# First MLP group of a gMLP/GLA layer step: up of two token blocks ahead of the third's, down by seven quadrant products, norm transposes later

## Chip, cores and metric

The kernel runs on one core of one Trainium2 chip. The metric is the device time of one launch in microseconds (us); the median of several launches counts.

## What is computed

One layer of an encoder step on 1056 tokens (1024 of a prompt, 32 of a running stream), model width 1024, all in fp32:

```python
def trunk_layer(x, c, s0, ...):
    mod = jax.nn.silu(c) @ w_ada + b_ada
    shift1, scale1, gate1, shift2, scale2, gate2 = split(mod, 6)
    h = x * (1.0 + scale1) + shift1
    mix, s_fin, v_rows = token_mixers(h, s0, ...)      # gated linear attention and gMLP
    x = layer_norm(DN_ALPHA * x + (1.0 + gate1) * (mix @ w_o + b_o), ln1_g, ln1_b)
    h2 = x * (1.0 + scale2) + shift2
    f = jnp.square(jax.nn.relu(h2 @ w_up + b_up)) @ w_down + b_down     # 1024 -> 4096 -> 1024
    x = layer_norm(DN_ALPHA * x + (1.0 + gate2) * f, ln2_g, ln2_b)
    return x, s_fin, v_rows
```

The change concerns the MLP (`w_up`, `w_down`) and what stands just ahead of it.

## The kernel before

**Tiles.** Tokens lie in three blocks: b = 0 and 1 of 384, b = 2 of 288 (256 and 32). Features lie on the partitions, so a tile of 128 features x 384 tokens is one matmul output. Every fp32 operand is split into a high and a low part (`hl`), and each product is three matmuls (`PASS`). A split is a CAST on ACT (L1024) and a subtraction on DVE (L1025).

**Stages around the change.** `out_proj_d(b)` computes the output projection (evicted to `y` by ACT, L936). `norm1(b)` turns `y` to rows (PE transposes, L1128), adds the residual, normalizes, turns back (PE transposes, L227), and forms `h2[b]`, eight feature tiles a block, as high and low part: ACT (L236) writes the high part, DVE (L233) the value, POOL (L239) the difference. Then the MLP runs in eight groups g of 512 of the 4096 features: up (1024 to 512, bias, relu, square) and down (512 to 1024, added into `acc`).

**Weights.** The class `W` loads raw weight tiles by DMA on SP (L1081) into four raw slots and splits them into eleven `hl` slots. A *unit* is 1024 numbers a partition in two slots. A *bundle* makes, from two units (A11, A12, A21, A22), also the sums that the Strassen-Winograd form needs (S1 to S4, on POOL, L1069 to L1072). `W.keep` holds slots back for others.

**Seven products.** In groups 1 to 7, blocks 0 and 1 are the two columns of a 2x2 matrix of quadrants, and up and down take seven products instead of eight (`Group.up` by the list `SEQ`, L1361; `Group.down` by `SEQ_DN`, L1428); block 2 is done plainly (`up_b2`, `down_b2`, L250 and L1222). The sums that up needs of `h2` (T1 to T4) are computed once by `t_prod` on POOL (L1257 to L1261), split, written to DRAM (`td`, by SP, L1267) and read back for each group through a ring of six slots (`ring`, issued by POOL, L1309). The sums that down needs of the group's own `f` are formed by `f_split`.

**Group 0** differs. Its up runs tile by tile through `up_std` (feature tiles m = 0, 1 for block 0, then for block 1, then block 2; then m = 2, 3 for all three), which squares on DVE (L1211) and splits f at once (L1212, L1213) into `f` and `fb2`. Its down is plain: for each of four weight units 12 matmuls for each of two outputs of each block (L1222), while `t_prod` makes the T products for the later groups.

**What sets the order.** PE's order is made by hand: `Order` runs generators by priority; each yields the PE time that it has issued and a delay until it wants its next turn (or a condition). `main_d` is the main stream, `norm1(b)` comes ahead of it when its delay has passed, `t_prod` behind it. The other engines are put in order when the program is built, by a scheduler that follows the tiles. Every engine then runs its queue strictly in that order.

Of the kernel before, what the change touches and what calls it, by code (L numbers as in the profile page):

```python
# [93 lines left out]
def cost(n):  # L94
    return max(n / 2.4, 106.0) + 2.0


def build(tc, io):
# [4 lines left out]
    with ctx:  # L103
# [9 lines left out]
        def mm():  # L113
            return cur["ps"].tile([P, 512], F32, tag="mm", name="mm", bufs=cur["mm"])
# [874 lines left out]
        with tc.tile_pool(name="pd", bufs=1, reuse_waits="tile") as pd, \  # L989
# [37 lines left out]
            class Weights:  # L1027
# [3 lines left out]
                def __init__(self):  # L1031
                    self.loads, self.steps, self.out, self.raw = [], [], {}, {}
                    self.keep = (0, 0)

# [39 lines left out]
                def pump(self):  # L1074
                    go = True
                    while go:
                        go = False
                        if self.loads and len(raws.free) > self.keep[0]:
                            key, u = self.loads.pop(0)
                            self.raw[key] = raws.take()  # L1080
                            DM.dma_start(self.raw[key], io["w"][u])  # L1081
                            go = True
                        if self.steps:
                            slot, f, k = self.steps[0]
                            if (k is None or k in self.raw) and (len(hls.free) > self.keep[1] if slot else halves.free):
# [23 lines left out]
            for m in range(4):  # L1109
                W.unit(("u", 0, m), U_UP + m)  # L1110
            for i in range(4):
                W.unit(("d", 0, i), U_DN + i)
            for g in range(1, 8):
                u, d = U_UP + 4 * g, U_DN + 4 * g
                W.bundle((("u", g, 0), (u, u + 2)), (("u", g, 1), (u + 1, u + 3)))
                if g < 7:
                    W.bundle(*((("d", g, r), (d + 2 * r, d + 2 * r + 1)) for r in range(2)))
                else:
                    for i in (0, 2, 1, 3):
                        W.unit(("d", 7, i), d + i)  # L1120
# [38 lines left out]
            def norm1(b):  # L1159
                tl = xr[b]  # L1160
                yield 0, 2500
                for wi, (off, n, _) in enumerate(WIN[b]):
# [38 lines left out]
            def up_std(hl, m, b, f):  # L1201
# [13 lines left out]
                yield from fm_tile(hl, h2[b], n, done)  # L1215

            def down_mm(pt, hl, q, f, n):

                for kk in range(4):
                    o_ = 256 * (kk % 2) + 128 * q  # L1220
                    for j, (a, c_) in enumerate(PASS):
                        PE.matmul(pt[:, :n], hl[kk // 2][:, a, o_:o_ + 128], f(kk)[:, c_],  # L1222
                                  start=(kk == 0 and j == 0), stop=(kk == 3 and j == 2))
# [22 lines left out]
            def t_prod():  # L1246

                yield lambda: h2[1] is not None
                for t, b, k0 in (("B11", 0, 0), ("B21", 0, 4), ("B22", 1, 4)):
                    for j in range(2):  # L1250
                        DM.dma_start(tv[t, j], h2[b][:, :, k0 + 2 * j:k0 + 2 * j + 2, :].bitcast(F32))
                for kk in range(4):
                    yield lambda: len(raws.free) >= 2 and len(hls.free) >= 2
                    r = [raws.take() for _ in range(2)]
                    b11, b12, b21, b22 = (r[i][:, 512 * j:512 * j + 384] for i in range(2) for j in range(2))
# [6 lines left out]
                    for t, src in (("T1", b11), ("T3", b12), ("T2", b22), ("T4", b21)):  # L1262
# [5 lines left out]
                        hls.give(h)  # L1268
                    for x_ in r:
                        raws.give(x_)  # L1270
                    yield 0, 9000
                W.keep = (0, 0)

# [27 lines left out]
            class Group:  # L1301
# [134 lines left out]
                def down_ev(self, prod, v, m):  # L1436
# [5 lines left out]
                    if prod == "P1":  # L1442
                        if self.g == 1:
# [86 lines left out]
            def main_d():  # L1530
# [14 lines left out]

                W.keep = (2, 3)
                yield lambda: h2[0] is not None
                tp = order.add(t_prod(), 7)
                f_a = [pd.tile([P, 2, 2, 768], F32R, tag="F", name="f", bufs=1)]

                def fa(m, b):
                    return f_a[m // 2][:, m % 2, :, 384 * b:384 * b + 384]
                hl = [W.unit_of("u", 0, m) for m in range(2)]
                for m in range(2):
                    yield from up_std(hl[m], m, 0, fa(m, 0))
                yield lambda: h2[1] is not None
                f_a.append(pd.tile([P, 2, 2, 768], F32R, tag="R", name="f", bufs=2))
                for m in range(2):
                    yield from up_std(hl[m], m, 1, fa(m, 1))
                yield lambda: h2[2] is not None  # L1560
                fb2 = pd.tile([P, 4, 2, 288], F32R, tag="R", name="fb2", bufs=2)
                for m in range(4):
                    if m > 1:
                        hl.append(W.unit_of("u", 0, m))
                        for b in range(2):
                            yield from up_std(hl[m], m, b, fa(m, b))
                    yield from up_std(hl[m], m, 2, fb2[:, m])
                    W.unit_done("u", 0, m)
# [4 lines left out]
                             .rearrange("p (a n) -> p a n", a=2) for i in range(3)]  # L1573
                groups = [Group(g) for g in range(8)]
                for gr in groups[1:]:
                    gr.queue()
                ring.pump()
                for i in range(4):
                    hl = W.unit_of("d", 0, i)
                    for b in range(3):  # L1580
                        for q in range(2):
                            pt = mm()
                            n = BLK[b][1]
                            down_mm(pt, hl, q, lambda kk: fb2[:, kk] if b == 2 else fa(kk, b), n)
                            down_ev(pt, 4 * (i % 2) + 2 * (i // 2) + q, ((b, 0, n),))
                            yield 12 * cost(n), 0
                    W.unit_done("d", 0, i)
                tmps_t = pd.tile([P, 8, 384], F32, tag="R", name="tmps", bufs=2)
                tmps = Slots([tmps_t[:, i] for i in range(6)])
                p1 = [tmps_t[:, 6], tmps_t[:, 7], pd.tile([P, 384], F32, name="p1")]  # L1590
                for g in range(1, 7):
# [111 lines left out]
```

## Time and profile before

| | us |
|---|---|
| three runs | 1233.87, 1240.7, 1239.12 (median 1239.12) |
| profiled execution | 1236.65, span 1234.9, mean granted clock 0.973 |
| busy: PE, weight load | 1171.4, 1116.4 |
| busy: DVE, ACT, POOL | 933.0, 531.9, 488.5 |
| 500 to 566 (group 0's up): PE busy, clock | 60.5 of 66, 0.87 |
| 566 to 612 (group 0's down): PE busy, clock | 46.0 of 46, 1.00 |
| 612 to 660 (group 1's up): PE busy, clock | 44.6 of 48, 0.96 |

Rows of a timeline give start, duration, engine, line, operation, output and inputs, shape, count; the brackets behind it give the idle time ahead of it and what ended that. Rows of windows give, after the stretch and its length, the busy time of PE, the weight load (PEld), DVE, ACT and POOL with their counts, then the granted TensorE clock (1.00 is full speed), the share of the DMA engines and GB/s. SPq is the DMA issue queue on SP.

### The profile page before, as it was taken

The numbers are of one execution on the slowest core, as the hardware profiler recorded it, in microseconds if no ns is written. First come the engines' busy times: TensorE is split into PE (matmuls) and PEld (weight loads), VectorE is DVE, ScalarE is ACT, GpSimd is POOL, SyncE is SP. The second block draws the span as 40 slices with busy tenths as digits, with TensorE's granted clock in tenths as the row PEclk, the third lists the DMA queues.
The fourth block names the chain that finished last, engine by engine and source line by source line (L and its number), as shares of the span: only waits on it lengthen the run. The fifth ranks groups of instructions, "written<-read, shape, count | busy, mean of one in ns | idle before, by whom it ended". The sixth has DMA issues, their size and how long they took to land.

```text
span 1234.9 us, 22104 instructions
## 1 busy us (share of the span) xinstructions
PE 1171.4 (95%) x8467; PEld 1116.4 (90%) x8467; DVE 933.0 (76%) x1906; ACT 531.9 (43%) x1087; POOL 488.5 (40%) x669
## 2 busy tenths in 40 slices
PE   5999997899899999899989999999999999999994
PEld 3679997798788899879989999999999999999994
DVE  5663899667888588767659769689598696796586
ACT  4462422544656577553334343343443443433221
POOL 3441224335665144448542442333324514432043
PEclk9999998899989999889999999999999999999998
DMA  9603456110102746304762563753825726637412
GB/s 373 222 2 133 154 207 219 50 37 3 40 2 72 279 126 227 126 18 150 264 251 69 195 242 97 242 180 117 301 94 190 254 79 216 234 102 248 146 49 93
DMA packets 49498, 188.46 MB, mean 153 GB/s; under 512 B 5328, under 2 KB 10928, under 8 KB 49392
## 3 DMA queue, kind: packets, MB, share of 16 engines
q1 hardware_dynamic: 35280, 109.97, 25.3%
q0 software_dynamic: 14112, 77.08, 18.0%
q8 instruction: 67, 1.10, 0.4%
q14 instruction: 39, 0.32, 0.1%
HBM read 171.36 MB, written 15.66 MB: 151 GB/s over the span
## 4 chain that ended last, share of the span: by engine, by line
PE 73%; DVE 12%; DMA 5%; POOL 3%; issue 2%; ACT 2%; SPq 0%; DVEq 0%; POOLq 0%; ACTq 0%
PE mm L250 22%; PE mm L1361 15%; PE mm L1428 13%; PE mm L1222 9%; PE zp L284 3%; PE mm L284 3%; DVE jk L883 2%; DVE hl L1025 2%; DMA raw<-in_w_dram 1%; DMA tdT<-hl 1%; DVE wad L883 1%; DMA wst<-in_w_dram 1%; DVE acc L1453 1%; PE zp L250 1%; PE mm L1128 1%
## 5 line engine op out<-in xcount | busy, mean ns | idle before, releaser
L1024 ACT CAST hl<-raw 128x512 fp32r<-128x512 f32 (+1 forms) x238 | 143.8, 613 | 238.8 <-PE mm L1428 94.6
L1025 DVE TENSOR_TENSOR hl<-raw,hl 128x512 fp32r<-128x512 f32 (+1 forms) x238 | 203.0, 859 | 36.5 <-ACT hl L1024 36.5
L1361 PE MATMUL mm<-ring,hl 128*128 128x384 f32 x960 | 172.8, 337 | 3.4 <-DMA ring<-tdT 3.4
L1361 PEld LDWEIGHTS mm<-ring,hl 128*128 128x128 f32 x960 | 167.7, 189 | 4.0 <-issue 3.2
L1428 PE MATMUL mm<-ring,hl 128*128 128x384 f32 x792 | 140.6, 335 | 1.1 <-DVE acc L1453 1.1
L1428 PEld LDWEIGHTS mm<-ring,hl 128*128 128x128 f32 x792 | 137.5, 188 | 1.4 <-ACT ring L1024 1.4
L250 PE MATMUL mm<-hT,whl 128*128 128x384 f32 (+1 forms) x792 | 132.3, 327 | 1.0 <-ACT mix L306 1.0
L250 PEld LDWEIGHTS mm<-hT,whl 128*128 128x128 f32 x792 | 129.7, 192 | 2.6 <-ACT mix L306 1.5
L250 PE MATMUL mm<-h,hl 128*128 128x288 f32 (+1 forms) x756 | 121.6, 317 | 1.9 <-POOL h L239 1.5
L250 PEld LDWEIGHTS mm<-h,hl 128*128 128x128 f32 x756 | 114.5, 195 | 4.8 <-POOL h L239 3.7
L1069 POOL TENSOR_TENSOR raw<-raw 128x512 f32<-128x512 f32 x26 | 37.2, 1432 | 183.6 <-DMA raw<-in_w_dram 161.3
L1453 DVE SCALAR_TENSOR_TENSOR acc<-mm,G,acc 128x384 f32<-128x384 f32 x162 | 93.8, 608 | 5.5 <-PE mm L1428 4.9
L1222 PE MATMUL mm<-fb,hl 128*128 128x288 f32 x708 | 97.0, 295 | 0.0
L1222 PEld LDWEIGHTS mm<-fb,hl 128*128 128x128 f32 x708 | 95.4, 189 | 0.0
L1233 DVE SCALAR_TENSOR_TENSOR acc<-mm,G,acc 128x256 f32<-128x256 f32 (+3 forms) x176 | 61.8, 390 | 12.3 <-PE mm L1222 12.2
L250 PE MATMUL mm<-mhl,hl 128*128 128x384 f32 (+1 forms) x384 | 65.1, 324 | 1.8 <-ACT hl L1024 1.8
L879 POOL TENSOR_TENSOR wad<-wad,csb 128x1024 f32<-128x1024 f32 x11 | 31.3, 2844 | 84.9 <-DVE jk L883 46.4
L284 PE MATMUL mm<-whl,hT 128*128 128x272 f32 (+1 forms) x384 | 55.3, 307 | 8.6 <-DVE whl L619 6.4
L284 PEld LDWEIGHTS mm<-whl,hT 128*128 128x128 f32 x384 | 53.2, 210 | 10.9 <-DVE whl L619 6.6
L250 PEld LDWEIGHTS mm<-mhl,hl 128*128 128x128 f32 x384 | 60.0, 192 | 2.6 <-ACT hl L1024 2.1
L1309 POOL DMA_DIRECT2D ring<-tdT x56 | 31.3, 560 | 73.0 <-PE mm L1361 42.1
L284 PE MATMUL zp<-zvw,hT 128*128 128x512 f32 x192 | 53.3, 423 | 4.5 <-ACT hT L236 4.5
(253 smaller groups left out, 2258.9 us busy)
## 6 DMA issues: line engine op xcount, KB each, us to landing
ring<-tdT POOLq DMA_DIRECT2D x56, 768.0 KB, 6.0
raw<-in_w_dram SPq DMA_DIRECT2D x80, 512.0 KB, 3.7
ring<-tdB POOLq DMA_DIRECT2D x42, 768.0 KB, 6.3
wst<-in_w_dram SPq DMA_DIRECT2D x34, 512.0 KB, 4.1
wad<-in_w_dram SPq DMA_DIRECT2D x32, 512.0 KB, 4.4
tdT<-hl SPq DMA_DIRECT2D x16, 384.0 KB, 3.0
st<-in_w_dram SPq DMA_DIRECT2D x10, 512.0 KB, 10.2
tdB<-h SPq DMA_DIRECT2D x6, 768.0 KB, 4.3
```

What stands on the lines that cost most here:

```text
L250: PE.matmul(pt[:, :n], h[:, a, 128 * kk:128 * kk + 128], act[:, b_, k, :n], start=(i == 0 and j == 0), stop=(i == 7 and j == 2))
L284: PE.matmul(pt[:n, :width], act[:, a, k, off:off + n], hl[:, b_, width * kk:width * kk + width], start=(k == 0 and a + b_ == 0), stop=(k = ...
L879: G.tensor_tensor(w, w, csb[:, c], ALU.mult)
L883: V.scalar_tensor_tensor(jk, w, 1.0, csb[:, c], ALU.mult, ALU.mult, accum_out=acc_)
L1024: S.copy(hl[:, 0, :n], src)
L1025: V.tensor_tensor(hl[:, 1, :n], src, hl[:, 0, :n].bitcast(F32), ALU.subtract)
L1069: G.tensor_tensor(s, a21, a22, ALU.add)
L1222: PE.matmul(pt[:, :n], hl[kk // 2][:, a, o_:o_ + 128], f(kk)[:, c_], start=(kk == 0 and j == 0), stop=(kk == 3 and j == 2))
L1233: V.scalar_tensor_tensor(ac, pt[:, o + lo - p0:o + hi - p0], G2[:, m, c:c + 1], ac, ALU.mult, ALU.add)
L1361: PE.matmul(pt[:, :384], hl[:, a, o_:o_ + 128], quad(ts[j])[:, b_, kk], start=first and j + kk + i == 0, stop=j + kk + i == 4, skip_group_ ...
L1428: PE.matmul(pt[:, :384], hl[:, a, o_:o_ + 128], f[:, b_, kk], start=first and kk + i == 0, stop=kk + i == 3, skip_group_check=True)
L1453: V.scalar_tensor_tensor(ac, v, G2[:, m, 0:1], ac, ALU.mult, ALU.add)
```

## The change

Group 0 now has the form of the later groups from its f on. Up of blocks 0 and 1 runs over all four feature tiles (`up_plain`: relu and square on ACT, f whole into one tile `F`), ahead of block 2's four tiles; down is `g0.down()`, which takes the seven products on `F` and block 2 plainly, first. Its four weight units become a bundle of two pairs (r = 0, 1); they may be loaded only after `t_prod` has taken two raw slots (`W.open`), and `t_prod` now keeps these two until all four of its steps kk are done. `norm1` waits twice as long before its first turn. `p1` (a product used in three places) is initialized by group 0 instead of group 1.

```diff
 def norm1(b):
     tl = xr[b]
-    yield 0, 2500
+    yield 0, 5000
...
+def up_plain(hl, m, b, f):
+    def done(pt):
+        t = tmp_tile("rl")
+        S.activation(t, pt[:, :384], AF.Relu, bias=col("b_up", m))
+        S.activation(f, t, AF.Square)
+    yield from fm_tile(hl, h2[b], 384, done)
...
# W: loading
-if self.loads and len(raws.free) > self.keep[0]:
+if self.loads and raws.free and (self.open or self.loads[0][0][0] != "d"):
...
-for i in range(4):
-    W.unit(("d", 0, i), U_DN + i)
-for g in range(1, 8):
+for g in range(8):
     u, d = U_UP + 4 * g, U_DN + 4 * g
-    W.bundle((("u", g, 0), (u, u + 2)), (("u", g, 1), (u + 1, u + 3)))
+    if g:
+        W.bundle((("u", g, 0), (u, u + 2)), (("u", g, 1), (u + 1, u + 3)))
     if g < 7:
         W.bundle(*((("d", g, r), (d + 2 * r, d + 2 * r + 1)) for r in range(2)))
...
# t_prod
+yield lambda: len(raws.free) >= 2
+r = [raws.take() for _ in range(2)]
+W.open = True
 for kk in range(4):
-    yield lambda: len(raws.free) >= 2 and len(hls.free) >= 2
-    r = [raws.take() for _ in range(2)]
+    yield lambda: len(hls.free) >= 2
...
-        for x_ in r:
-            raws.give(x_)
         yield 0, 9000
-W.keep = (0, 0)
+for x_ in r:
+    raws.give(x_)
+W.keep = 0
...
# main_d, after the output projection
-W.keep = (2, 3)
+W.keep = 3
...
-hl = [W.unit_of("u", 0, m) for m in range(2)]
-for m in range(2):
-    yield from up_std(hl[m], m, 0, fa(m, 0))
-yield lambda: h2[1] is not None
...
-for m in range(2):
-    yield from up_std(hl[m], m, 1, fa(m, 1))
+g0.f = pd.tile([P, 4, 768], F32, tag="F", name="F", bufs=1)
+hl = []
+for ms in ((0, 1), (2, 3)):
+    hl += [W.unit_of("u", 0, m) for m in ms]
+    for b in range(2):
+        yield lambda: h2[b] is not None
+        for m in ms:
+            yield from up_plain(hl[m], m, b, g0.f[:, m, 384 * b:384 * b + 384])
...
 for m in range(4):
-    if m > 1:
-        hl.append(W.unit_of("u", 0, m))
-        for b in range(2):
-            yield from up_std(hl[m], m, b, fa(m, b))
     yield from up_std(hl[m], m, 2, fb2[:, m])
     W.unit_done("u", 0, m)
 yield lambda: tp not in order.streams
...
-for i in range(4):
-    hl = W.unit_of("d", 0, i)
-    for b in range(3):
-        for q in range(2):
-            pt = mm()
-            n = BLK[b][1]
-            down_mm(pt, hl, q, lambda kk: fb2[:, kk] if b == 2 else fa(kk, b), n)
-            down_ev(pt, 4 * (i % 2) + 2 * (i // 2) + q, ((b, 0, n),))
-            yield 12 * cost(n), 0
-    W.unit_done("d", 0, i)
+yield from g0.down()
 for g in range(1, 7):
     yield from groups[g].up()
     yield from groups[g].down()
```

Lines behind the change move by some nine: L1222, L1257 to L1261, L1267, L1309, L1361 and L1428 are L1229, L1266 to L1270, L1276, L1318, L1370 and L1437 in the changed kernel; L1128, L1155, L1207 and L1211 to L1213 are one lower.

Three places of the order. First PE, where the third block's rows are turned back (L227; 2 + 1 transposes a feature tile). Before (`h_5881` is h2[1], `h_6191` h2[2]):

```order
L250 MATMUL mm<-h_5881,hl_5130 128x384 x12
L250 MATMUL mm<-h_5881,hl_5127 128x384 x12
L227 MATMUL mm<-ident,xr 128x128 x2
L227 MATMUL mm<-ident,xr 128x32
...
L250 MATMUL mm<-h_6191,hl_5137 128x288 x12
L250 MATMUL mm<-h_6191,hl_5131 128x288 x12
```

Changed (`h_5449` is h2[0]):

```order
L250 MATMUL mm<-h_5449,hl_5121 128x384 x12
L227 MATMUL mm<-ident,xr 128x128 x2
L227 MATMUL mm<-ident,xr 128x32
L250 MATMUL mm<-h_5449,hl_5122 128x384 x6
...
L227 MATMUL mm<-ident,xr 128x128 x2
L227 MATMUL mm<-ident,xr 128x32
L250 MATMUL mm<-h_5901,hl_5121 128x384 x6
...
L250 MATMUL mm<-h_5901,hl_5124 128x384 x12
L250 MATMUL mm<-h_6184,hl_5137 128x288 x12
```

The eight sets of transposes stood in one run ahead of the third block's up; they now stand singly between half tiles of blocks 0 and 1, and the third block's up follows behind m = 3.

Second POOL, at the affines of block 1 (L239, output h2[1]: `h_5881` before, `h_5901` changed). Before:

```order
L239 TENSOR_TENSOR h_5881<-t_5982,h_5881 128x384
L239 TENSOR_TENSOR h_5881<-t_6014,h_5881 128x384
L217 TENSOR_SCALAR rs<-mv 128x1
L218 TENSOR_TENSOR rs<-rs,mhalf 128x1
L239 TENSOR_TENSOR h_5881<-t_6029,h_5881 128x384
L217 TENSOR_SCALAR rs<-mv 128x1
L218 TENSOR_TENSOR rs<-rs,mhalf 128x1
L239 TENSOR_TENSOR h_5881<-t_6049,h_5881 128x384
```

Changed:

```order
L239 TENSOR_TENSOR h_5901<-t_5907,h_5901 128x384
L1266 TENSOR_TENSOR raw_5133<-h_5449 128x384
L1069 TENSOR_TENSOR raw_5135<-raw_5129 128x512
L1266 TENSOR_TENSOR raw_5134<-h_5901 128x384
L239 TENSOR_TENSOR h_5901<-t_5930,h_5901 128x384
L239 TENSOR_TENSOR h_5901<-t_5947,h_5901 128x384
L1267 TENSOR_TENSOR raw_5134<-raw_5134 128x384
L239 TENSOR_TENSOR h_5901<-t_5962,h_5901 128x384
L239 TENSOR_TENSOR h_5901<-t_5977,h_5901 128x384
L1266 TENSOR_TENSOR raw_5133<-h_5901 128x384
L217 TENSOR_SCALAR rs<-mv 128x1
L1268 TENSOR_TENSOR raw_5134<-raw_5133,raw_5134 128x384
```

t_prod's sums (L1266 to L1270) and the first sum of the down weights (L1069, of the raw tile 5129) now stand among the affines.

Third SP, at the loads of group 0's down weights. Before, the four units (the first four rows) are issued ahead of t_prod's writes to DRAM (L1267, `tdT`); the other two loads are group 1's:

```order
L1081 DMA raw_5134<-in_w_dram 128x1024
L1081 DMA raw_5128<-in_w_dram 128x1024
L1081 DMA raw_5133<-in_w_dram 128x1024
L1081 DMA raw_5129<-in_w_dram 128x1024
L1081 DMA raw_5133<-in_w_dram 128x1024
L1251 DMA tdB_5150<-h_5881 256x1x768
L1251 DMA tdB_5151<-h_5881 256x1x768
L1081 DMA raw_5134<-in_w_dram 128x1024
L1267 DMA tdT_5146<-hl_5122 256x1x384
```

Changed: the first pair of units is loaded ahead of the `tdT` writes, and the second pair (`raw_5134` and `raw_5133`, t_prod's own slots until then) at their end:

```order
L1276 DMA tdT_5149<-hl_5125 256x1x384
L1276 DMA tdT_5147<-hl_5126 256x1x384
L1276 DMA tdT_5145<-hl_5136 256x1x384
L1081 DMA raw_5134<-in_w_dram 128x1024
L1276 DMA tdT_5141<-hl_5137 256x1x384
L1276 DMA tdT_5149<-hl_5131 256x1x384
L1081 DMA raw_5133<-in_w_dram 128x1024
```

More of the change, by code (lines that the diff above doesn't have):

```diff
@@ L1032, in __init__ @@
                     self.loads, self.steps, self.out, self.raw = [], [], {}, {}
-                    self.keep = (0, 0)
+                    self.keep, self.open = 0, False
                 def unit(self, key, u):
@@ L1084, in pump @@
                             slot, f, k = self.steps[0]
-                            if (k is None or k in self.raw) and (len(hls.free) > self.keep[1] if slot else halves.free):
+                            if (k is None or k in self.raw) and (len(hls.free) > self.keep if slot else halves.free):
                                 self.steps.pop(0)
@@ L1305, in queue @@
                 def queue(self):
-                    for _, _, t, _, _ in SEQ:
+                    for _, _, t, _, _ in SEQ if self.g else ():
                         for j in range(2):
@@ L1442, in down_ev @@
                     if prod == "P1":
-                        if self.g == 1:
+                        if self.g == 0:
                             S.copy(p1[m], v)
@@ L1544, in main_d @@
                 order.add(norm1(2), 0)
-                W.keep = (2, 3)
+                W.keep = 3
                 yield lambda: h2[0] is not None
                 tp = order.add(t_prod(), 7)
-                f_a = [pd.tile([P, 2, 2, 768], F32R, tag="F", name="f", bufs=1)]
-                def fa(m, b):
-                    return f_a[m // 2][:, m % 2, :, 384 * b:384 * b + 384]
-                hl = [W.unit_of("u", 0, m) for m in range(2)]
-                for m in range(2):
-                    yield from up_std(hl[m], m, 0, fa(m, 0))
-                yield lambda: h2[1] is not None
-                f_a.append(pd.tile([P, 2, 2, 768], F32R, tag="R", name="f", bufs=2))
-                for m in range(2):
-                    yield from up_std(hl[m], m, 1, fa(m, 1))
+                groups = [Group(g) for g in range(8)]
+                g0 = groups[0]
+                g0.f = pd.tile([P, 4, 768], F32, tag="F", name="F", bufs=1)
[6 more added lines that the diff above has]
+                            yield from up_plain(hl[m], m, b, g0.f[:, m, 384 * b:384 * b + 384])
+                g0.have |= {"C11", "C12", "C21", "C22"}
+                tmps_t = pd.tile([P, 8, 384], F32, tag="R", name="tmps", bufs=2)
+                tmps = Slots([tmps_t[:, i] for i in range(6)])
+                p1 = [tmps_t[:, 6], tmps_t[:, 7], pd.tile([P, 384], F32, name="p1")]
                 yield lambda: h2[2] is not None
@@ L1573, in main_d @@
                              .rearrange("p (a n) -> p a n", a=2) for i in range(3)]
-                groups = [Group(g) for g in range(8)]
-                for gr in groups[1:]:
+                for gr in groups:
                     gr.queue()
                 ring.pump()
-                for i in range(4):
-                    hl = W.unit_of("d", 0, i)
-                    for b in range(3):
-                        for q in range(2):
-                            pt = mm()
-                            n = BLK[b][1]
-                            down_mm(pt, hl, q, lambda kk: fb2[:, kk] if b == 2 else fa(kk, b), n)
-                            down_ev(pt, 4 * (i % 2) + 2 * (i // 2) + q, ((b, 0, n),))
-                            yield 12 * cost(n), 0
-                    W.unit_done("d", 0, i)
-                tmps_t = pd.tile([P, 8, 384], F32, tag="R", name="tmps", bufs=2)
-                tmps = Slots([tmps_t[:, i] for i in range(6)])
-                p1 = [tmps_t[:, 6], tmps_t[:, 7], pd.tile([P, 384], F32, name="p1")]
+                yield from g0.down()
                 for g in range(1, 7):
```

## Prediction

> **What bounds the kernel now.** I read the page's busy list and chain first, then the windows around the change, then the timelines of PE, ACT and POOL there.
>
> ```profile
> PE 1171.4 (95%) x8467; PEld 1116.4 (90%) x8467; DVE 933.0 (76%) x1906; ACT 531.9 (43%) x1087; POOL 488.5 (40%) x669
> ...
> PE 73%; DVE 12%; DMA 5%; POOL 3%; issue 2%; ACT 2%; SPq 0%; DVEq 0%; POOLq 0%; ACTq 0%
> ```
>
> ```profile
> 500.00:566.00 66.00, 60.51 (x329) 55.32 (x328) 44.26 (x84) 36.36 (x72) 29.31 (x33) 0.87 0.19 69
> 566.00:612.00 46.00, 46.00 (x289) 46.00 (x288) 32.09 (x51) 12.48 (x24) 31.65 (x31) 1.00 0.68 246
> ```
>
> PE holds 73% of the chain, so a microsecond counts where it is taken from PE's work or from a wait in front of PE. The windows (length; busy us of PE, weight load, DVE, ACT, POOL; granted clock) say that the stage being rewritten has both kinds: from 500 to 566, the first group's up tiles, PE idles 5.5 us and runs at a clock of 0.87; from 566 to 612, its down, PE is full. There only fewer matmuls help, and any new wait is paid in full. The PE timeline (start, us, ..., the wait ahead in brackets):
>
> ```profile
> 452.12 0.33 PE L227 MATMUL mm<-ident,xr 128*128 128x128 f32 x1 [0.97 <-ACT xr L1169]
> ...
> 471.31 0.33 PE L1128 MATMUL mm<-ident,y 128*128 128x128 f32 x1 [1.09 <-ACT y L936]
> ...
> 497.57 0.49 PE L227 MATMUL mm<-ident,xr 128*128 128x128 f32 x3
> 497.82 1.29 PE L250 MATMUL mm<-h,hl 128*128 128x384 f32 x6
> ...
> 503.94 0.48 PE L1128 MATMUL mm<-ident,y 128*128 128x128 f32 x1 [3.62 <-ACT y L936]
> ...
> 516.88 7.53 PE L250 MATMUL mm<-h,hl 128*128 128x384 f32 x42
> 524.25 4.35 PE L227 MATMUL mm<-ident,xr 128*128 128x128 f32 x24
> ...
> 537.42 28.76 PE L250 MATMUL mm<-h,hl 128*128 128x288 f32 x173 [0.26 <-POOL h L239]
> 566.02 8.49 PE L1222 MATMUL mm<-f,hl 128*128 128x384 f32 x48
> 574.34 3.37 PE L1222 MATMUL mm<-fb,hl 128*128 128x288 f32 x24
> 577.54 8.52 PE L1222 MATMUL mm<-f,hl 128*128 128x384 f32 x48
> ...
> 612.23 4.96 PE L250 MATMUL mm<-h,hl 128*128 128x288 f32 x36
> ...
> 638.35 1.31 PE L1361 MATMUL mm<-ring,hl 128*128 128x384 f32 x6 [2.92 <-DMA ring<-tdT]
> 640.14 4.78 PE L1361 MATMUL mm<-ring,hl 128*128 128x384 f32 x18 [0.48 <-DMA ring<-tdT]
> ```
>
> Starts give the pace: (574.34 − 566.02)/48 = 0.1733 us a matmul of 384 tokens, (577.54 − 574.34)/24 = 0.1333 us one of 288. Three transposes set between matmuls cost 497.82 − 497.57 = 0.25 us. The clock in these stretches (same columns):
>
> ```profile
> 504.00:508.00 4.00, 4.00 (x15) 3.90 (x16) 4.00 (x8) 2.62 (x5) 2.45 (x3) 0.50 0.39 131
> 508.00:512.00 4.00, 4.00 (x23) 3.87 (x23) 2.71 (x6) 2.38 (x4) 2.96 (x5) 0.75 0.13 50
> ...
> 530.00:538.00 8.00, 6.55 (x17) 4.38 (x18) 6.35 (x17) 7.41 (x20) 4.70 (x7) 0.53 0.18 66
> ```
>
> So a gap of 3.62 us costs PE about 4 × 0.50 + 4 × 0.25 = 3.0 us more at a lower clock.
>
> **What is removed.** (1) The 3.62 us gap. ACT explains it:
>
> ```profile
> 502.29 1.14 ACT L1024 CAST hl<-raw 128x512 fp32r<-128x512 f32 x2 [1.73 <-DMA raw<-in_w_dram]
> 503.33 0.83 ACT L936 ACTIVATE y<-mm,gb,G 128x256 f32<-128x256 f32 x2
> ```
>
> The eviction of y stands behind the split of a down weight whose load is late. Down weights are now closed until t_prod has taken its slots, so that split leaves the place: −3.62 − 3.0 = **−6.6**. (2) The gaps at 452 and 471: the transposes of norm1 come later behind their producer. **−2.1**. (3) From 524.25 to 566.02 are 41.8 us; in it lie 96 matmuls of 384 (16.6) and 96 of 288 (12.8), and 24 transposes that would cost 8 × 0.25 = 2.0 if they stood between matmuls, as they now do. The rest, 41.8 − 31.4, is the wait for the third block: **−10.4**. (4) Down of the two 384-token blocks: 4 units × 48 = 192 matmuls become 7 products × 24 = 168: 24 × 0.1733 = **−4.2**. (5) The ring wait at 638: 2.92 + 0.48, and 1.31 + 4.78 − 24 × 0.1733 = 1.9 of slow matmuls: **−5.3**. T products are now all written some tens of us ahead of the second group. If nothing replaced these, the sum would be −28.6.
>
> The work moved to DVE and ACT (f split into seven operands, 27 evictions where 16 stood, eight more weight splits) lies in the down window, where these two are busy 32.1 and 12.5 of 46 us; I cost it at nothing as long as what follows sets the pace. Its upper end is what one more DVE wait would cost PE there, about 3 us.
>
> **What is added.** Both new waits come from POOL, so its prices are needed: POOL's timeline, the raw tiles' groups (duration ns min/median/max), and that tile's landing time:
>
> ```profile
> 517.36 1.01 POOL L239 TENSOR_TENSOR h<-t,h 128x384 fp32r<-128x384 f32 x1
> ...
> 572.75 4.55 POOL L1257 TENSOR_TENSOR raw<-h 128x384 f32<-128x384 f32 x4
> ...
> 581.89 4.57 POOL L1257 TENSOR_TENSOR raw<-h 128x384 f32<-128x384 f32 x4
> ```
>
> ```profile
> L1024 ACT CAST hl<-raw x50: 503/615/632, 470.1 to 618.4; 128x512 fp32r<-128x512 f32 x34, 128x384 fp32r<-128x384 f32 x16
> L1025 DVE TENSOR_TENSOR hl<-raw,hl x49: 545/694/2872, 469.4 to 618.7; 128x512 fp32r<-128x512 f32 x33, 128x384 fp32r<-128x384 f32 x16
> ...
> L1069 POOL TENSOR_TENSOR raw<-raw x3: 1268/1287/1694, 538.6 to 619.9; 128x512 f32<-128x512 f32 x3
> ...
> L1072 POOL TENSOR_TENSOR raw<-raw x2: 1741/1745/1749, 616.4 to 618.1; 128x512 f32<-128x512 f32 x2
> ...
> DMA to landing us min/median/max: 3.4/3.6/10.4
> ```
>
> Eight t_prod operations follow each other in 581.89 − 572.75 = 9.14 us, 1.14 each.
>
> (6) *The second block's affines.* Before, POOL does the eight affines of h2[1] alone (the last ends at 518.4) and starts t_prod at 540. Now nine t_prod operations and one weight sum (L1069) stand among them. Eight affines × 1.0, nine × 1.14, 1.3, and four small norm operations of some 0.5: 21.5 us. The first affine comes at about 501 (2.5 us of later transposes), so the last ends near 522.5, and the first tile of block 1, whose last matmuls need it, near 523.5. Before, this tile ended at 524.41 − 24 × 0.1733 = 520.2 (the x42 row less block 1's second tile); without gaps (1) and (2) PE would be done at 511.5. The new wait is **+12.0**. It trickles in affine by affine, as from 530 to 538, where the clock was 0.53; I add **+2.0** for that (low end 0; high end 4 us, half rate for those 8 us). Low end of the wait: 5 us, if affines and t_prod overlap with waits that POOL has anyway; high end 15, since L1069 waits for a weight load in POOL's queue.
>
> Then 120 matmuls of 384 (20.8) and the interleaved transposes (2.0) run, and the third block's up begins at X = 523.5 + 2.0 + 22.8 = 548.3; it ends at X + 12.8 = 561.1, 4.9 ahead of before.
>
> (7) *The late half of the down weights.* t_prod keeps both of its raw slots until all four k are done, and from its second k on its splits need weight slots that only the third block's up tiles free, the first at X + 3.2. POOL has 18 t_prod operations and three weight sums from X + 4.4 (a split is 0.5 + 0.7): 18 × 1.14 + 3 × 1.745 = 25.8, to X + 30.2. Split 1.2, load 3.6: the second pair of down weights lands at X + 33 to X + 35 and the first of it is split by X + 34.3. Third-block down with the first pair needs PE from X + 12.8 to X + 19.2 (48 × 0.1333); it also waits within this for the last fb2 tile, about 4 us, behind splits that wait for T transfers on ACT. In all PE idles 34.3 − 19.2 = **+15.1**, and takes **+3.0** of slow clock after it (as in row 503.94). Then 6.4 + 3.0 + 168 × 0.1733 = 38.5: the second group starts at X + 72.8 = 621.1 against 612.23. Low end of the wait: 6 us, if T splits find slots earlier; high end 20, if a load takes the 10.4 of the landing row's maximum.
>
> **Sum.** −28.6 + 12.0 + 2.0 + 15.1 + 3.0 = +3.5. The profiled execution took 1236.65, so 1240.1; it stands 2.5 below the median of the three runs (1239.12; 1233.87 to 1240.7), and I put the median run at **1241.5**.
>
> On the clock, the Trainium skill (TensorE: Matmul & The Clock Gate, "What's actually happening") has half rate after one idle window of about 3.4 us and full rate after as long a busy one. By it a gap would cost 1.7 and the two new ones 3.4 instead of my 5.0, a sum of +1.9; the trace shows about 6 us of lower clock after 503.94, and the measured row stands in the sum. The same page ("PE-mode transpose") says that transposes don't count as busy; the 0.53 from 530 to 538, after 24 transposes in a row and with waits under half a microsecond each, agrees, and speaks for the interleaving in (3).
>
> **Rivals.** A: *POOL isn't the bound, faster.* If t_prod finds slots while PE is still at the two blocks, the sums end before X + 19 and PE never sees them; (6) shrinks to its low end as well. For it: POOL was busy only 29.3 of 66 us in that window. Against it: its order is fixed by the program, and an idle POOL waits with it. With the low ends 5 + 0 + 6 + 3, the sum is −14.6, a run of 1222 to 1225; from about half of both waits on it is measurably faster.
>
> B: *ACT's queue stretches (7), slower.* ACT now has splits of the first down pair that wait for T transfers, and behind them the T splits that POOL waits for:
>
> ```profile
> ACT hl L1024 <- DMA tdT<-hl: 13.2, 5, 6.1
> ```
>
> Five such waits cost 13.2 us before, hidden by a full PE. If four of them (2.6 each) fall into the chain from X + 4.4, the sum is +14, a run of 1252; from one on it passes +0.5%.
>
> C: *cancels, the forecast*: the new waits take what the old ones give, within some 6 us.
>
> **Chances.** 0.5% (6.2 us) is about what a measurement here tells from no change. C 0.44: the prices are rows, the places are in the program's order; of it 0.32 within 0.5%, 0.04 faster, 0.08 slower. A 0.26 (0.24 faster, 0.02 same): the old losses are certain, the new ones worked out. B 0.30 (0.28 slower, 0.02 same). Faster 0.28, same 0.36, slower 0.36. The range 1226 to 1254 leaves out the lower half of A and the tail of B; C alone would give 1235 to 1248.
>
> **What would show it.** Step by step: no wait on y near 500 and a clock near 1 there (1); the third block's transposes in threes between matmuls and no wait ahead of its up (3); 168 matmuls at 0.173 in the products (4); no ring wait in the second group's first T products (5); the last L239 of h2[1] at 520 to 525 with t_prod among the others, PE waiting for POOL h (6); a PE wait of 10 to 18 us in the third block's down, on ACT or DVE hl, with raw loads landing some 33 us after the third block's up began (7). Wrong I am if PE meets no wait in (7), or if POOL is ahead of PE in (6): then the run is 15 us or more faster.

## Result and profile after

The changed kernel is slower: 1248.73 us, median of six launches (1245.85 to 1251.02), against 1234.24 for the kernel before beside it; ratio 1.010 (1.008 to 1.012). The profiled execution took 1250.42, span 1248.7. Its page, busy list and chain:

```profile
PE 1166.4 (93%) x8443; PEld 1111.7 (89%) x8443; DVE 949.5 (76%) x1923; ACT 543.5 (44%) x1102; POOL 496.6 (40%) x677
...
PE 72%; DVE 15%; issue 3%; DMA 3%; POOL 3%; ACT 2%; SPq 0%; DVEq 0%; ACTq 0%; POOLq 0%
```

PE does less (24 matmuls, 5 us) and the span grows by 13.8: the loss is waiting. DVE's share of the chain goes from 12 to 15%. The windows say where (columns as for the kernel before):

```profile
500.00:566.00 66.00, 56.85 (x342) 52.96 (x340) 42.22 (x71) 38.32 (x76) 44.35 (x47) 0.94 0.23 84
566.00:612.00 46.00, 28.09 (x151) 26.51 (x151) 39.66 (x59) 20.00 (x35) 21.64 (x18) 0.75 0.38 130
```

The down stage that had a full PE (46.0 of 46) now has one busy for 28.1. PE's timeline:

```profile
457.12 0.33 PE L227 MATMUL mm<-ident,xr 128*128 128x128 f32 x1 [1.94 <-ACT xr L1168]
...
520.35 8.82 PE L250 MATMUL mm<-h,hl 128*128 128x384 f32 x38 [2.80 <-POOL h L239]
529.01 0.56 PE L227 MATMUL mm<-ident,xr 128*128 128x128 f32 x3
529.49 1.32 PE L250 MATMUL mm<-h,hl 128*128 128x384 f32 x6
530.65 0.55 PE L227 MATMUL mm<-ident,xr 128*128 128x128 f32 x3
...
540.98 20.34 PE L250 MATMUL mm<-h,hl 128*128 128x384 f32 x138
561.16 0.97 PE L1229 MATMUL mm<-fb,hl 128*128 128x288 f32 x6
565.54 0.61 PE L1229 MATMUL mm<-fb,hl 128*128 128x288 f32 x1 [3.41 <-ACT fb L1211]
568.39 0.85 PE L1229 MATMUL mm<-fb,hl 128*128 128x288 f32 x2 [2.25 <-DVE fb L1212]
...
572.27 6.87 PE L1229 MATMUL mm<-fb,hl 128*128 128x288 f32 x38 [1.17 <-DVE fb L1212]
591.48 6.87 PE L1229 MATMUL mm<-fb,hl 128*128 128x288 f32 x32 [12.34 <-ACT hl L1024]
...
601.47 15.16 PE L1437 MATMUL mm<-ring,hl 128*128 128x384 f32 x84
...
631.03 6.55 PE L250 MATMUL mm<-h,hl 128*128 128x288 f32 x48
```

The reader sees the second block's wait for POOL at 520, the transposes in threes, a third block's up without a wait, and then two kinds of wait in the down: for the third block's own f, `fb2` (565 to 572, 8.1 us in four waits) and, 12.3 us, for the second pair of down weights. No ring wait is left in the second group.

**Stages.** Executions of one kernel differ by some us before PE reaches the change: its first matmul on `mhl` and a rotating weight (`mm<-mhl,hl`, ahead of the output projection) starts anywhere from 420.7 to 426.5. So I compare from that start on. Each number is the difference of two starts in a PE timeline: first down matmul of group 0, first matmul of the second group, its first down matmul, end of the span.

| kernel | up to group 0's down | group 0's down | second group's up | rest | sum |
|---|---|---|---|---|---|
| before | 141.7 | 46.2 | 47.2 | 575.4 | 810.6 |
| changed | 136.0 | 69.9 | 41.9 | 575.8 | 823.5 |
| changed (e9) | 135.8 | 69.4 | 41.9 | 576.0 | 823.1 |
| e1 up order alone | 128.3 | 46.5 | 51.6 | 575.6 | 802.0 |
| e12 the same again | 129.0 | 46.2 | 51.6 | 576.1 | 803.0 |
| e8 the same, delay 2500 | 131.7 | 46.2 | 53.6 | 575.9 | 807.5 |
| e2 products alone | 153.7 | 49.3 | 41.9 | 577.0 | 821.9 |
| e3 own weight slots | 141.7 | 60.3 | 41.9 | 575.4 | 819.3 |
| e4 few T sums | 132.5 | 51.9 | 41.9 | 575.5 | 801.8 |
| e5 own slots, f splits later | 140.2 | 51.7 | 41.9 | 575.8 | 809.6 |
| e6 f splits later | 134.9 | 68.6 | 41.9 | 575.7 | 821.2 |
| e7 affines first | 131.3 | 70.2 | 41.9 | 575.7 | 819.1 |
| e10 the same again | 134.3 | 70.2 | 42.0 | 575.8 | 822.3 |
| e11 all three mends | 134.2 | 58.9 | 41.9 | 576.1 | 811.1 |

The change gives 5.7 in the up, 5.3 in the second group's up, and loses 23.7 in group 0's down. The rest of the program is the same to 0.4 us. How far one profile can be trusted shows in e7 and e10, which are one and the same kernel: their sums differ by 3.2, nearly all of it in the up.

### The profile page after: what moved, and what is told of

Same layout as the page of the kernel before. It is cut to its first block, busy times and chain, and to the rows that moved or that the text cites. A ratio compares the mean times of both kernels' runs of the same rounds, so it can differ in the third digit from the quotient of the medians.

```text
span 1248.7 us, 22107 instructions
## 1 busy us (share of the span) xinstructions
PE 1166.4 (93%) x8443; PEld 1111.7 (89%) x8443; DVE 949.5 (76%) x1923; ACT 543.5 (44%) x1102; POOL 496.6 (40%) x677
## 4 chain that ended last, share of the span: by engine, by line
PE 72%; DVE 15%; issue 3%; DMA 3%; POOL 3%; ACT 2%; SPq 0%; DVEq 0%; ACTq 0%; POOLq 0%
PE mm L250 19%; PE mm L1370 16%; PE mm L1437 14%; PE mm L1229 10%; PE zp L284 3%; DVE jk L883 3%; DVE hl L1025 2%; PE mm L284 2%; DMA raw<-in_w_dram 2%; DVE wad L883 1%; DVE acc L1462 1%; DMA wst<-in_w_dram 1%; PE zp L250 1%; PE gt L763 1%; DMA wad<-in_w_dram 1%
## 5 line engine op out<-in xcount | busy, mean ns | idle before, releaser
L1025 DVE TENSOR_TENSOR hl<-raw,hl 128x512 fp32r<-128x512 f32 (+1 forms) x240 | 197.1, 829 | 20.8 <-ACT hl L1024 20.8
L1437 PE MATMUL mm<-ring,hl 128*128 128x384 f32 x924 | 165.3, 335 | 1.2 <-DVE acc L1462 1.1
L1437 PEld LDWEIGHTS mm<-ring,hl 128*128 128x128 f32 x924 | 160.4, 188 | 2.2 <-ACT hl L1024 1.4
L1370 PE MATMUL mm<-ring,hl 128*128 128x384 f32 x912 | 161.7, 334 | 0.0
L1370 PEld LDWEIGHTS mm<-ring,hl 128*128 128x128 f32 x912 | 158.0, 188 | 0.0
L250 PE MATMUL mm<-h,hl 128*128 128x288 f32 (+1 forms) x804 | 124.5, 310 | 4.2 <-POOL h L239 3.1
L250 PEld LDWEIGHTS mm<-h,hl 128*128 128x128 f32 x804 | 117.5, 190 | 5.5 <-POOL h L239 3.6
L1069 POOL TENSOR_TENSOR raw<-raw 128x512 f32<-128x512 f32 x28 | 38.2, 1363 | 201.8 <-DMA raw<-in_w_dram 166.9
L1462 DVE SCALAR_TENSOR_TENSOR acc<-mm,G,acc 128x384 f32<-128x384 f32 x189 | 109.3, 607 | 5.7 <-PE mm L1437 4.9
L1229 PE MATMUL mm<-fb,hl 128*128 128x288 f32 x624 | 93.4, 305 | 21.3 <-ACT hl L1024 12.3
L1229 PEld LDWEIGHTS mm<-fb,hl 128*128 128x128 f32 x624 | 88.7, 197 | 23.3 <-ACT hl L1024 12.6
L1240 DVE SCALAR_TENSOR_TENSOR acc<-mm,G,acc 128x256 f32<-128x256 f32 (+2 forms) x160 | 52.2, 366 | 12.8 <-PE mm L1229 12.7
L1340 ACT CAST ring<-F 128x768 fp32r<-128x768 f32 x49 | 40.8, 836 | 45.1 <-DVE F L1332 18.9
L1318 POOL DMA_DIRECT2D ring<-tdT x56 | 31.5, 563 | 68.1 <-PE mm L1370 42.8
```

What stands on the lines that cost most here:

```text
L250: PE.matmul(pt[:, :n], h[:, a, 128 * kk:128 * kk + 128], act[:, b_, k, :n], start=(i == 0 and j == 0), stop=(i == 7 and j == 2))
L1025: V.tensor_tensor(hl[:, 1, :n], src, hl[:, 0, :n].bitcast(F32), ALU.subtract)
L1069: G.tensor_tensor(s, a21, a22, ALU.add)
L1240: V.scalar_tensor_tensor(ac, pt[:, o + lo - p0:o + hi - p0], G2[:, m, c:c + 1], ac, ALU.mult, ALU.add)
L1340: S.copy(q[:, 0], src)
L1370: PE.matmul(pt[:, :384], hl[:, a, o_:o_ + 128], quad(ts[j])[:, b_, kk], start=first and j + kk + i == 0, stop=j + kk + i == 4, skip_group_ ...
```

## Experiments

The theory is that of the prediction: POOL's T sums, and the weight slots and raw slots that `t_prod` holds, delay first the second block's affines and then the second pair of down weights.

**e1: the new up order alone.** Kernel before, `norm1` at 5000, the new order of the up tiles, plain down.

```diff
-hl = [W.unit_of("u", 0, m) for m in range(2)]
...
+for ms in ((0, 1), (2, 3)):
+    hl += [W.unit_of("u", 0, m) for m in ms]
+    for b in range(2):
...
+        for m in ms:
+            yield from up_std(hl[m], m, b, fa(m, b))
```

> The kernel before with one part of the change alone: up of blocks 0 and 1 over all four feature tiles ahead of the third block's, and the norm delay of 5000; down stays plain (four units), weights and t_prod as before. Theory (the new up order is a gain, the seven products are what costs): the wait for the third block, 10.4 us, is gone, the ring wait of the second group (5.3) stays; 1220 to 1228 us against 1234, the third block's up without a wait ahead of it. Rival (the transposes between the half tiles cost as much elsewhere, the up order is no gain): 1231 to 1237.

Measured 1226.15 (1224.41 to 1231.23), ratio 0.992 (0.989 to 0.995): faster than both kernels. PE's timeline, its only wait between 456 and the second group, and the largest in that group:

```profile
502.83 1.30 PE L250 MATMUL mm<-h,hl 128*128 128x384 f32 x6 [1.20 <-DVE acc L1185]
...
615.38 7.67 PE L1361 MATMUL mm<-ring,hl 128*128 128x384 f32 x34 [3.43 <-DVE hl L1025]
```

This is the theory's number. The old waits of the up are worth 13.4 us (12.7 in e12), and they go with the order of the up tiles and the norm delay together; e8 tells the two apart. Of this 4.4 come back in the second group, whose weights and T products are now wanted earlier.

**e2: the products alone.** Changed kernel with the old up order and 2500.

> The changed kernel with the up order of before (feature tiles 0 and 1 for the three blocks, then 2 and 3) and the norm delay of 2500; down by seven products, weights and t_prod as in the change. Theory (t_prod's splits wait for the slots that the third block's up frees): here the first of these come free earlier, T sums are mixed among the affines of both blocks and end near 560, so the wait in the down shrinks below 5 us, and a wait for the third block's affines of 10 to 20 us takes its place; 1234 to 1242 us. Rival (the products with t_prod's held raw slots cost what they cost in the changed kernel, wherever up stands): 1247 to 1255 us with a wait of 10 us or more in the down.

Measured 1246.49 (1244.88 to 1250.04), ratio 1.008 (1.005 to 1.011). The time lies between the two forecasts. The up gets 12.0 us longer than before, the down some 3 longer: with the old order the T sums meet the affines of both later blocks. PE's timeline shows two waits on y, the one on the second block's affines (519.51), the largest of seven on the third block's (546.04; 9.5 us in all) and the larger on f:

```profile
498.42 0.66 PE L1127 MATMUL mm<-ident,y 128*128 128x128 f32 x4 [0.81 <-ACT y L936]
...
500.59 0.33 PE L1127 MATMUL mm<-ident,y 128*128 128x128 f32 x1 [0.59 <-ACT y L936]
...
519.51 6.26 PE L250 MATMUL mm<-h,hl 128*128 128x384 f32 x26 [4.20 <-POOL h L239]
...
546.04 2.27 PE L250 MATMUL mm<-h,hl 128*128 128x288 f32 x6 [2.29 <-POOL h L239]
...
582.32 0.61 PE L1229 MATMUL mm<-fb,hl 128*128 128x288 f32 x1 [3.64 <-ACT fb L1211]
```

There is no late weight here, and still the sum is 11 above before: under the old order too, the products' work on POOL costs PE where POOL's affines stand in the same queue.

**e4: few T sums.** Changed kernel with the POOL sums of three of the four kk left out (their T products are not computed).

```diff
...
+if kk == 0:
+    G.tensor_tensor(b11, b12, b11, ALU.subtract)
...
```

> The changed kernel without t_prod's POOL sums of three of its four steps kk (24 of 32 operations; the T products written are those of the first step). Splits, DMAs, slots and held raw tiles are as in the change. Theory (POOL's sums behind the third block's up are the length of the late chain): the chain loses some 20 us, the second pair of down weights is there about when PE wants it; 1226 to 1234 us. Rival (the chain is slots, splits on ACT and DVE and T transfers, and POOL only follows it): 1243 us or more.

Measured 1225.73 (1224.93 to 1226.52), ratio 0.991 (0.989 to 0.993). The 12 us wait is gone and the f waits are smaller:

```profile
560.28 0.61 PE L1229 MATMUL mm<-fb,hl 128*128 128x288 f32 x1 [1.76 <-ACT fb L1211]
...
564.16 14.17 PE L1229 MATMUL mm<-fb,hl 128*128 128x288 f32 x86 [2.03 <-DVE fb L1212]
```

So 24 POOL sums, 27 us of POOL time at 1.14, cost the whole program 22 us (823.5 − 801.8). The run shows what the sums cost, and not by which way: without them POOL's queue is shorter, and DVE runs undisturbed too (last section). Even without them the sum of stages (801.8) is only that of e1 (802.0): the products gain nothing here that the up order alone doesn't.

**e3: own weight slots.** `t_prod` takes three weight slots with its raw slots and rotates in them, so its splits no longer wait for slots of the up weights.

```diff
+own = Slots([hls.take() for _ in range(3)])
...
-        h = hls.take()
+        h = own.take()
```

> The changed kernel, but t_prod takes three split slots for itself at its start and uses them in turn, so that its splits don't wait for slots that the third block's up frees. Theory (those slots put the 18 late sums and with them the second pair of down weights behind the third block's up): the sums end near 560, the wait for the second pair of down weights falls from 12.3 us to under 5, some 5 to 10 us of wait for block 2's affines come up ahead of its up; 1222 to 1232 us. Rival (POOL's total of work or the held raw slots set the end, not the split slots): the wait only moves, 1240 us or more.

Measured 1244.8 (1242.67 to 1246.59), ratio 1.007 (1.004 to 1.009): the number is the rival's, and the gain was expected at least some four times as large. The sums end at 553.5 and the wait for weights is gone, but the waits for f, hidden behind it until now, grow in its place. PE's timeline, then DVE's ahead of the largest:

```profile
570.01 0.66 PE L1229 MATMUL mm<-fb,hl 128*128 128x288 f32 x3 [2.50 <-DVE fb L1212]
574.79 0.85 PE L1229 MATMUL mm<-fb,hl 128*128 128x288 f32 x2 [4.11 <-DVE fb L1212]
...
582.89 0.61 PE L1229 MATMUL mm<-fb,hl 128*128 128x288 f32 x1 [2.61 <-ACT fb L1211]
```

```profile
569.51 0.45 DVE L1212 TENSOR_TENSOR fb<-rl,fb 128x288 fp32r<-128x288 f32 x1
569.88 0.94 DVE L1336 TENSOR_TENSOR F<-F 128x768 f32<-128x768 f32 x1
570.75 1.88 DVE L1025 TENSOR_TENSOR hl<-raw,hl 128x512 fp32r<-128x512 f32 x3
572.55 0.94 DVE L1334 TENSOR_TENSOR F<-F 128x768 f32<-128x768 f32 x1
573.42 0.94 DVE L1340 TENSOR_TENSOR ring<-F,ring 128x768 fp32r<-128x768 f32 x1
574.29 0.44 DVE L1212 TENSOR_TENSOR fb<-rl,fb 128x288 fp32r<-128x288 f32 x1
```

Between two splits that PE waits for, DVE does 4.4 us that PE doesn't need yet: sums of f (L1334, L1336), a split of f for the products (L1340), weight splits (L1025). The weight splits among them are for the second pair, which PE takes only after these. POOL lost time as well: the sums now stand among the third block's affines (2.28 us of PE ahead of 554.72), and the up is 5.7 longer than in the changed kernel, more than half of the 9.6 that the down gains.

**e5: own slots, and f splits later.** As e3, with the splits and sums of group 0's f held behind the third block's last `fb2` split on ACT and DVE.

```diff
+with tc.issue_after(fb_last[0]), tc.issue_after(fb_last[1]):
+    self.f_split(t, s)
```

> The kernel with t_prod's own three split slots, and the group's f splits for the products (six sums and subtractions on DVE, their casts on ACT) queued behind the third block's last fb2 tile on ACT and DVE. With its own slots alone the kernel waited in front of the third block's down 2.5, 4.1, 1.2, 2.0, 2.6 and 1.0 us for fb2. Theory (what is left of the loss is DVE's queue: fb2 stands behind the f splits and the weight splits): those waits fall from 13.4 us to 3 to 7, and 1244.8 us become 1234 to 1239. Rival (fb2 waits for the weight splits on DVE or for ACT, and the f splits only fill idle time): 1242 to 1247, or slower, since the products wait for f.

Measured 1233.26 (1231.01 to 1236.13), ratio 0.998 (0.997 to 1.000); 8.6 of e3's down go:

```profile
569.27 0.61 PE L1231 MATMUL mm<-fb,hl 128*128 128x288 f32 x1 [2.23 <-ACT fb L1213]
571.63 13.65 PE L1231 MATMUL mm<-fb,hl 128*128 128x288 f32 x86 [1.75 <-DVE fb L1214]
585.12 14.73 PE L1444 MATMUL mm<-ring,hl 128*128 128x384 f32 x84
```

Nothing was removed, the rows of DVE and ACT only changed places: order in a queue is what more than half of e3's waits were. The two mends together undo the loss of the change but make no gain over before.

**e6: f splits later, without own slots.** Changed kernel with the f splits behind `t_prod`'s last split, by the same means.

> The changed kernel with the f splits of group 0 queued behind t_prod's last split on ACT and DVE. In the changed kernel the split of t_prod's last T3 waited on ACT from 578.5 to 583.6 us behind a cast of f, and with it the load of the second pair of down weights. Theory (ACT's queue stretches the late chain by this): the load is issued 5 to 8 us earlier, the wait of 12.3 us falls to 4 to 8, 1240 to 1245 us against 1248.7. Rival (the f splits fill time in which the chain waits anyway, and now delay the products): 1247 to 1253.

Measured 1245.69 (1244.32 to 1249.06), ratio 1.008 (1.006 to 1.011). PE's timeline:

```profile
581.86 7.42 PE L1231 MATMUL mm<-fb,hl 128*128 128x288 f32 x32 [7.29 <-ACT hl L1026]
...
601.43 9.14 PE L1448 MATMUL mm<-ring,hl 128*128 128x384 f32 x42 [1.89 <-DVE acc L1473]
```

The second pair comes 25.5 us after the first down matmul (556.35) instead of 30.3 (561.16 to 591.48), so 4.8 of its lateness was the f splits ahead of the last T splits. But the f splits, now later themselves, slow the products: 1.89 us on DVE, and 32.9 us for them instead of 29.6. Only 1.3 of the stage is won.

**e7 and e10: affines first.** Changed kernel with the T sums on POOL held behind the last affine of block 1.

```diff
+es_.enter_context(tc.issue_after(aff_last[1]))
```

> The changed kernel with t_prod's POOL sums queued behind the last affine of the second block's h2. Theory (the sums among the affines hold block 1's first tile by 8 to 12 us): PE's waits of 1.1 and 2.8 us near 517 and 520 and the half clock after them go, the third block's up begins 7 to 10 us earlier than 548.3, and since the late chain starts from it, the time falls as much: 1238 to 1242 us. Rival (the late chain does not hang on the third block's up, so what is won here is waited for in the down): 1245 to 1250.

> The changed kernel with the T sums on POOL behind the last affine of the second block (as in e7, whose profile ended its up tiles 7.3 us earlier while its median was only about 1 us lower). Theory (the wait for the affines, 4 to 5 us with its low clock, is paid in full by the whole program, and the late chain starts from the third block's up, so it moves along): 6 to 8 us below the changed kernel of this batch. Rival (the affine wait is hidden behind the late weights, so nothing is gained): within 2 us of it.

e7: 1247.69 (1243.37 to 1250.65), ratio 1.009 (1.006 to 1.012). e10: 1245.13 (1243.32 to 1250.61), ratio 1.008 (1.006 to 1.011), beside 1250.40 for the changed kernel (e9). The intervals overlap. e7's median is the rival's number; e10's lies 5.3 below e9, between the two forecasts. By the stages the up gains 4.7 in one profile, which caught the fastest of e7's launches, and 1.5 in the other, the slowest of e10's, so the gain stays uncertain. What remains is seen in e7's PE timeline, and in its POOL timeline:

```profile
518.55 0.33 PE L227 MATMUL mm<-ident,xr 128*128 128x128 f32 x1 [0.95 <-ACT xr L1170]
520.50 0.24 PE L227 MATMUL mm<-ident,xr 32*128 32x32 f32 x1 [1.63 <-ACT xr L1170]
```

```profile
509.93 3.93 POOL L1270 TENSOR_TENSOR raw<-h 128x384 f32<-128x384 f32 x4
513.83 0.21 POOL L217 TENSOR_SCALAR rs<-mv 128x1 f32<-128x1 f32 x1
...
515.14 0.56 POOL L218 TENSOR_TENSOR rs<-rs,mhalf 128x1 f32<-128x1 f32 x1
```

The sums no longer stand ahead of block 1's affines, but now ahead of the small operations of the third block's norm, on which its transposes wait: the first of them (L217 at 513.83) had its input from DVE (L216) at 510.0. In the down nothing changes (70.2 each): the late chain starts from the third block's up and moves with it.

The changed kernel in the same batch as e10:

> The changed kernel once more, unaltered, so that the three other runs of this batch have it on the same chip. Both theories: 1245 to 1251, PE idle 4.3 us for POOL's affines between 515 and 521, third block's up from 548 on, and one wait of about 12 us for the second pair of down weights.

Measured 1250.40 (1245.85 to 1251.04), ratio 1.011 (1.008 to 1.013), with the same waits and the same stages to 0.4 us.

**e8: the new up order with delay 2500.** As e1 without the longer delay.

> The kernel before with the new up order of group 0 alone (1226.2 us with the norm delay of 5000), and the norm delay of before, 2500. Theory (the later norm transposes are worth little: in the changed kernel one of the two gaps in front of them went, the other grew from 0.97 to 1.94): 1223 to 1230 us. Rival (the delay is what took the gap of 3.6 us away): 1231 us or more, with a wait on y of 2 us or more near 503.

Measured 1233.71 (1230.72 to 1238.24), ratio 0.998 (0.996 to 0.999).

```profile
500.24 0.47 PE L1128 MATMUL mm<-ident,y 128*128 128x128 f32 x1 [3.72 <-ACT y L936]
```

This is the rival's number and its sign: the y gap (term 1) is back, and the order alone is worth 0.2% where the order with the longer delay is worth 0.8%. In e1, where the down weights are as open as in the kernel before, the longer norm delay alone removed it; in e2, with closed weights and the short delay, 0.81 and 0.59 of it are left. So the delay alone takes it away wholly; in e2 another part of the change takes most of it, which may be the weights that the prediction named.

**e11 and e12: all mends together, and e1 again.**

> The changed kernel with all three mends: three own weight slots for the T splits, group 0's f splits behind the third block's last f split on ACT and DVE, T sums behind the second block's last affine on POOL. Theory (three waits, each a queue's order, make up the loss, and they are separate): e5's 1233.3 less the affine waits that its PE timeline shows (0.26 + 1.10 + 3.17 = 4.5, and slow clock behind them), so 1226 to 1230. Rival (the T sums that come later on POOL run into the third block's up and stretch DVE and the second pair's loads again): 1233 or more.

> The kernel before with the new up order and the norm transposes at 5000 alone, as in e1, in more rounds and beside e11. Both theories: 1224 to 1228, 0.5 to 1.1% below the kernel before. It tells whether the products, once mended (e11), are worth anything beyond the new up order: theory (their 24 fewer matmuls, 4.2 us, and the ring wait of 5 us are paid for by work on DVE, ACT and POOL): e11 not below e12. Rival (mended, they bring the 9 us that the sum gave them): e11 4 us or more below e12.

e11: 1235.25 (1232.78 to 1236.81), ratio 0.999 (0.998 to 1.001). e12: 1226.62 (1225.39 to 1228.93), ratio 0.993 (0.991 to 0.995). e11 wins 6.0 over e5 in the up and loses 7.2 in the down. Its products take 34.3 us where e5's took 29.1, and PE's timeline has a wait there that e5 doesn't:

```profile
591.83 9.34 PE L1449 MATMUL mm<-ring,hl 128*128 128x384 f32 x42 [3.10 <-DVE acc L1474]
```

For e11 the rival had it: what was won at the affines is paid later, in front of the products. The fastest version that computes the whole layer is e1 (e12), 0.7 to 0.8% below the kernel before; the seven products of group 0 don't pay in any form tried. Own slots that leave the affines alone, joined to e1's up, were not tried.

## Why the prediction was off

The time lay in the range, 7 us above the number, and on the side of slower instead of no change. That it lies no further off is in part luck: the number stood on a kernel before of 1239.12, and beside the changed kernel it took 1234.24. The change itself was forecast as +3.5, and it is +14.5 (1248.73 − 1234.24), or +12.9 by the stages.

**What came as worked out.** 24 matmuls fewer: 168 products in 631.03 − 601.47 = 29.6 us against 29.1 (4). The ring wait: 5.3 gained, 5.3 forecast (5). The third block's up began without a wait, at 561.16 − 12.8 = 548.4, forecast 548.3. POOL's 18 late sums and three weight sums ended at 580.6, 32.2 us behind that, against 30.2. The slow clock after the long wait (columns as above):

```profile
591.00:595.00 4.00, 3.52 (x13) 3.30 (x14) 2.11 (x4) 1.56 (x3) 0.00 (x0) 0.50 0.99 339
595.00:599.00 4.00, 3.35 (x20) 3.04 (x19) 3.06 (x4) 2.08 (x4) 2.85 (x3) 0.84 0.46 164
```

While PE was busy again it cost 3.52 × 0.50 + 4 × 0.16 = 2.4 against 3.0. One busy window of some 3.4 us at half rate, as the Trainium skill has it (TensorE: Matmul & The Clock Gate, "What's actually happening"), would have made it 1.7; the rows lie halfway between the two, by their clocks some 4.8 us of half rate from 591.48 on. That section also calls the window free-running, so one such figure doesn't fit every gap. The prediction's sum by that figure, +1.9, has a slip: at 1.7 a gap, the gap (1) that goes would cost less too, and the sum is +3.2.

**Two terms that were each too large, and cancelled.** Removed waits (1) to (3) were put at 19.1; e1 shows 13.4. The norm gap (2) didn't go (1.94 at 457 where two gaps of 0.97 and 1.09 were). A set of transposes between half tiles costs 530.65 − 529.01 − 6 × 0.1733 = 0.60, not 0.25: 2.8 us over eight (0.25 was also read too low, since the kernel before has 498.94 − 497.57 − 6 × 0.1733 = 0.33). And 1.2 us came at 503 on DVE. The affine wait with its clock (6) was put at 14.0 and is 7.7 (136.0 − 128.3). I read the two as one, which no run separates: POOL set when block 1 was ready, so whatever PE arrived later by, it waited less. The net, −5.7, was forecast as −5.1; that it came so near is luck. The sign of (6) did come: the last affine of block 1 ended at 520.3, with T sums among the others. Term (6) also named only half of the cause: e7 and e10 take the sums away from the affines, and the third block's norm, on the same queue, sets the end next. Of (1) the gap did go, and the cause given is one of two (e8).

**The step that failed is (7)**, and with it the sentence that costs the moved DVE and ACT work at nothing. The weights came late in the way that (7) describes, but the stage was sized too small: with (4) the down was to get 13.9 longer, and it got 23.7 longer. Group 0's down was forecast at 60.0 and took 69.9. PE went on with the second pair 591.48 − 548.4 = 43 us after the third block's up began, not 34.3. Two of these nine are POOL's. The others lie between POOL's last sum and the split weight, 10.9 us where 4.1 were counted. ACT, then SP's queue:

```profile
582.87 0.83 ACT L1340 CAST ring<-F 128x768 fp32r<-128x768 f32 x1 [3.52 <-DVE F L1333]
583.60 0.92 ACT L1024 CAST hl<-raw 128x384 fp32r<-128x384 f32 x2
...
590.80 1.14 ACT L1024 CAST hl<-raw 128x512 fp32r<-128x512 f32 x2 [0.93 <-DMA raw<-in_w_dram]
```

```profile
562.48 24.17 SPq L1276 DMA_DIRECT2D tdT<-hl  x6
586.74 0.56 SPq L1081 DMA_DIRECT2D raw<-in_w_dram  x1
```

The last T splits (583.60) stand on ACT behind a cast of f (L1340) that waits 3.52 us for an f sum on DVE; only then does SP write the T product and issue the load. e6 takes that order away and the pair comes 4.8 earlier. What makes the weights late, the slots and the sums, is shown by e3 (own slots, no wait for weights) and by e4 (few sums). That is rival B's kind of mechanism, a queue that stretches (7), but through f casts rather than the T transfers it named.

Behind it stood a second loss that the first one hid: the waits for `fb2`, 8.1 us here, which the prediction gave "about 4" and at most 3 us of cost. With the weights in time (e3) these waits are 13.4 us in six, and e5 shows that more than half of that is order in the queues of DVE and ACT. For the 8.1 in the changed kernel there is a second candidate, which no run takes apart from the first: DVE beside POOL's sums (last section).

## What to carry to other kernels

Before work is moved onto an engine that is half idle, write down its queue there: what PE will wait for stands behind whatever was issued first, and a busy share of 32 of 46 us says nothing about that. When two changes come together, cost them apart: here the reordering with the longer norm delay was worth 0.8%, and the algebra with fewer matmuls lost more than that. A mend that removes the largest wait uncovers the next one, so size the waits that it hides before counting the gain.

## What the hardware showed

DVE's two-input operations take two and a half to three times as long beside a POOL sum. DVE and POOL timelines of the changed kernel (POOL is idle from 570.83 to 571.92):

```profile
554.33 1.27 DVE L1212 TENSOR_TENSOR fb<-rl,fb 128x288 fp32r<-128x288 f32 x1
555.52 1.37 DVE L1025 TENSOR_TENSOR hl<-raw,hl 128x384 fp32r<-128x384 f32 x1
556.81 0.44 DVE L1210 TENSOR_TENSOR rl<-rl 128x288 f32<-128x288 f32 x1
...
571.77 0.45 DVE L1212 TENSOR_TENSOR fb<-rl,fb 128x288 fp32r<-128x288 f32 x1
```

```profile
555.24 1.23 POOL L1266 TENSOR_TENSOR raw<-h 128x384 f32<-128x384 f32 x1
557.03 1.10 POOL L1266 TENSOR_TENSOR raw<-h 128x384 f32<-128x384 f32 x1 [0.56 <-DVE hl L1025]
```

The subtraction at 555.52 ends at 556.89, 0.42 behind the POOL sum that ends at 556.47; the multiplication at 556.81, in POOL's gap of 0.56, takes 0.44. The same split of f takes 1.27 beside the sums and 0.45 where it starts in a gap of POOL. So a stretch of 18 POOL sums is also a stretch of slow DVE, and POOL in turn waits for DVE's splits (0.56 ahead of 557.03). The Trainium skill (SBUF — State Buffer, "Who interferes with whom") says that a DVE instruction with two SBUF inputs contends with a GpSimd one that reads SBUF, and that the port pair they share is an exclusive lock; these rows agree. From 559.66 to 571.77 DVE works without a gap on eleven such operations, in 12.1 us. At the times that the same shapes take without a POOL sum beside them (1.88 for three of 128x512 in e3, 0.45 for 128x288, 0.55 for 128x384) they would take about 6.3, by estimate, and PE's waits for `fb2` fall in just this stretch. How much of the waits, or of the nine late microseconds, this makes was not measured by itself.
